# A second spare pair for split weights in the down projection of a hybrid decoder layer

## The chip, the cores and the metric

The kernel runs on one core of a Trainium2 chip. The core has five engines with instruction queues of their own: TensorE (PE in the profile; its weight loads are PEld), VectorE (DVE), ScalarE (ACT), GpSimd (POOL) and SyncE (SP), of which the last two issue transfers here. An engine takes its instructions in the order of the program and waits on semaphores. The metric is the time of one execution on the device, in microseconds; the median of three runs before is 2103.13 us (2101.62 to 2104.65).

## The reference

One decoder layer on x of 512 tokens by 2048, all in float32. With a token mixer (gated linear attention in 4 heads and differential attention in 4 heads) and a gated MLP:

```
h = rmsnorm(x, attn_pre_norm)
x = x + rmsnorm(token_mixer(h, ...), attn_post_norm)
h = rmsnorm(x, ffn_pre_norm)
up = h @ w_ffn_in                      # 2048 x 11264
a, b = up[..., :5632], up[..., 5632:]
a = conv_w[0]*a[t-2] + conv_w[1]*a[t-1] + conv_w[2]*a[t] + conv_b
f = (gelu(a) * b) @ w_ffn_out          # 5632 x 2048: the down projection
y = x + rmsnorm(f, ffn_post_norm)
```

The change concerns the last product, `@ w_ffn_out`.

## The kernel before

**Split weights.** TensorE works on operands of a rounded type (float32r). To keep float32 accuracy, each operand is split in two: ScalarE copies the raw tile into a rounded high half (line 137), VectorE subtracts that from the raw tile and writes the low half (line 138). A product is then three matmuls: high by high, high by low, low by high (lines 1348 to 1350 in the down projection). The unit of this work is the *granule*: 128 x 1024 weights, loaded in one transfer, split by one instruction on each of the two engines, and used by twelve matmuls of 128 x 512. `granule` does it, and takes the place of the two halves either from a *ring* of three slots (`halves`) or from a *spare pair* (`spare_halves`; tiles xhi and xlo, allocated once and kept in `kept`). Before TensorE has read a slot to the end, the next granule that has this slot can't be split. With every fourth granule in the spare pair, the ring and the pair make four slots in turn.

**The down projection.** The 11 groups of 512 hidden columns are taken as five pairs and one single group (`last_group`, at the end). Each pair, for each half of the 2048 output columns, is one *unit*: ten units, 0 to 9. A unit is a product of 2 x 2 blocks computed with seven block products instead of eight. Its segments are, in order, x0, z0, y0, z1, x1, y1, y2, of two granules each, so 14 granules or 168 matmuls; the order between units is chained (`x0` and `z0` of the next unit stand before and behind `y2` of this one). In this text 1/z0/0 is unit 1, segment z0, granule 0. The raw weights of a unit lie in three pairs of tiles: `rt` (segments x0, z0, y0, y2), a first pair of `raw` (z1, y1), and a second pair of `raw` (x1). Between its uses a tile is changed in place: after x0 and after z1 GpSimd issues a transfer that adds another weight block to it (`accum_op`, line 1194, and line 1454 in the hand-ordered part); before y0 and before y2 VectorE adds a `raw` tile to it (lines 1211 and 1229). The other operand of the products, the activations, comes from DRAM tiles `sd` as `st`, and is split into `ah` and `al` by ScalarE and VectorE (lines 150 and 151, a *preparation*); seven preparations belong to each pair of groups, so they fall between an odd unit and the even unit behind it. After each segment the banks are added to four accumulators `acc` (ScalarE copies the first of them, line 1354; VectorE adds, line 1356).

**What sets the order.** The step from the up projection to unit 1 is written by hand: `run_in_order` in a manual schedule, which ends with 0/y2/1. It takes its own list of spare granules (a local name `extra`), with every fourth granule of its later part in the spare pair; its last granule is one of these. From 1/z0/0 on, the flag `extra[0]` is set and the framework's scheduler orders each engine's instructions itself, by a model of their times, from the dependencies that the program order and the tiles give. `Unit.run` counts granules in `turn[0]` and asks for the spare pair.

**Tiles of the large pool.** Tiles of 128 x 2048 come from a pool of six places (tag t8). The up projection holds six split sums there; the four accumulators take four of the places at the change-over, and `g3` (the last norm's weights, 1 MB, loaded on SP's queue) takes the next free one.

Of the kernel before, what the change touches and what calls it, by code (L numbers as in the profile page):

```python
# [10 lines left out]
F32R = mybir.dt.float32r  # L11
# [19 lines left out]
GR = 1024  # L31
# [4 lines left out]
def hybrid_layer(ctx: ExitStack, tc: tile.TileContext, x, attn_pre_norm, w_in, w_alpha_up, b_alpha,  # L36
# [4 lines left out]
    x2, out2 = x[0], out[0]  # L41
# [58 lines left out]
    def load(src, a, by=None):  # L100
        raw = wpool.tile([P, GR], F32, name="raw", tag="raw", bufs=4)
        (by or nc.sync).dma_start(out=raw.rearrange("p (a b) -> p a b", a=a), in_=src)
        return raw
# [9 lines left out]
    def halves():  # L113
        slot[0] = (slot[0] + 1) % 3
        return [ring[:, RS * i + p:RS * i + p + GR] for i, p in zip((slot[0], slot[0] + 3), place_w[0])]

    kept = []

    def spare_halves(pool):
        if pool == "rt":  # L120
            return [rp.tile([P, GR], F32R, name=n, tag="rt", bufs=4) for n in ("xhi", "xlo")]
        if pool is True:
            if not kept:
                kept.extend(small_tile(n, F32R) for n in ("xhi", "xlo"))
            return kept
        return [pool.tile([P, GR], F32R, name=n, tag=n, bufs=4) for n in ("xhi", "xlo")]

    def granule(src, a, raw=None, spare=None, hl=None):
        if raw is None:
            raw = load(src, a)  # L130
        if hl is not None:
            hi, lo = hl[:, 0, :], hl[:, 1, :]
        elif spare:
            hi, lo = spare_halves(spare)
        else:
            hi, lo = halves()
        act(hi, raw, AF.Copy)  # L137
        tt(lo, raw, hi.bitcast(F32), ALU.subtract)  # L138
        r = "p (a b) -> p a b"
        return hi.rearrange(r, a=a), lo.rearrange(r, a=a)  # L140
# [932 lines left out]
    def small_tile(name, dt=F32):  # L1073
        return fp.tile([P, GR], dt, name=name, tag="t4", bufs=6)

    def large_tile(name, dt=F32):
        return fp.tile([P, D], dt, name=name, tag="t8", bufs=6)
# [88 lines left out]
    turn = [0]  # L1166
    extra = [False]

    class Unit:
# [12 lines left out]
        def run(self, seg, op, raws):  # L1182
            c, first = self.where(seg)
            if first:
                self.banks[c] = self.chain(c)
            for g in range(2):
                turn[0] += 1
                place_w[0] = APART if self.a == 4 else LEVEL
                hl = granule(None, self.a, raws[g], spare=extra[0] and turn[0] % 4 == 0)
                self.prods(self.banks[c], op, g, hl, first)  # L1190

        def more(self, raws, j):
# [464 lines left out]
```

## Time and profile before

| What | Value |
|---|---|
| median of the runs (lowest to highest) | 2103.13 us (2101.62 to 2104.65) |
| the profiled execution's own time | 2106.11 us |
| its span (first to last instruction) | 2104.4 us |
| mean granted clock of TensorE | 0.996 |
| TensorE busy between 1700 and 1800 us | 97.09 of 100 us |
| TensorE busy between 1800 and 1900 us | 98.75 of 100 us |
| TensorE busy between 1900 and 2000 us | 96.60 of 100 us |
| VectorE busy in these three stretches | 84.40, 82.05, 85.90 us |
| ScalarE busy in these three stretches | 51.91, 43.89, 44.51 us |

The profile shows one execution, in microseconds from the start of its span. A row of a timeline gives the start, the duration, the engine, the line, the operation, what it writes and reads, the count of equal instructions in a row, and in brackets the idle time of the engine before it with what ended it. A row of waits gives who waited for whom, then the total, the number and the longest. A row of stretches gives the length, then the busy time of PE, PEld, DVE, ACT and POOL with instruction counts, then the granted clock of TensorE (1.00 is full speed), the mean busy share of the DMA engines, and GB/s. Matmuls overlap: of two rows in a row the starts count, not the durations.

### The profile page before, as it was taken

What the parts mean: (1) busy time and instruction counts of PE and PEld (TensorE: products, weight loads), DVE (VectorE), ACT (ScalarE), POOL (GpSimd) and SP (SyncE); (2) the same over time, 40 slices, a digit from 0 to 9 for tenths busy, and PEclk for the clock granted to TensorE, in tenths of its full rate; (3) what the DMA queues carried; (4) which work ended last, traced back from release to release, by engine and by line L of the source; (5) the groups of instructions that cost most, each with busy time, mean ns of one, the idle gap of its engine ahead of it and who ended that gap; (6) DMA issues with size and microseconds to landing.
All of it is one profiled execution on the core that took longest, in us unless ns stands there. A gap on an engine that the chain in (4) does not pass through costs nothing.

```text
span 2104.4 us, 35571 instructions
## 1 busy us (share of the span) xinstructions
PE 2062.8 (98%) x14449; PEld 1903.4 (90%) x14449; DVE 1507.9 (72%) x1802; ACT 1001.9 (48%) x1306; POOL 287.5 (14%) x306
## 2 busy tenths in 40 slices
PE   7999999999989999999999999999999999999998
PEld 6699999999988889899999999999999878787786
DVE  5967777676752255986777767777777778888877
ACT  4544444455742233454554545455455554444443
POOL 0112222322200000011111011111111110110100
PEclk9999999999999999999999999999999999999999
DMA  5488887878875344447668577567676876776663
GB/s 210 118 185 179 191 197 176 178 176 198 196 193 175 100 150 161 140 103 196 150 147 196 140 162 190 135 163 175 164 160 179 239 208 168 192 189 159 171 169 140
DMA packets 280696, 358.60 MB, mean 170 GB/s; under 512 B 14592, under 2 KB 221876, under 8 KB 278612
## 3 DMA queue, kind: packets, MB, share of 16 engines
q1 hardware_dynamic: 191380, 259.85, 37.1%
q0 software_dynamic: 84800, 94.38, 29.6%
q8 instruction: 113, 1.85, 0.4%
q10 hardware_dynamic: 4352, 2.10, 0.3%
q14 instruction: 51, 0.42, 0.1%
HBM read 311.72 MB, written 44.56 MB: 169 GB/s over the span
## 4 chain that ended last, share of the span: by engine, by line
issue 37%; PE 29%; POOL 3%; DMA 2%; DVE 2%; ACT 1%; POOLq 0%; DVEq 0%; ACTq 0%; SPq 0%
PE bank L1248 4%; PE bank L1247 4%; PE bank L1246 4%; PE bank L191 3%; PE bank L192 3%; PE bank L193 3%; POOL raw L1194 1%; POOL rt L1194 1%; PE bank L1349 1%; PE bank L1350 1%; PE bank L1348 1%; PE bank L1553 1%; PE bank L1554 1%; PE bank L1552 1%; PE bank L175 1%
## 5 line engine op out<-in xcount | busy, mean ns | idle before, releaser
L138 DVE TENSOR_TENSOR ring<-raw,ring 128x1024 fp32r<-128x1024 f32 x315 | 383.1, 1221 | 280.8 <-ACT ring L137 276.5
L137 ACT ACTIVATE ring<-raw 128x1024 fp32r<-128x1024 f32 x315 | 333.3, 1060 | 516.4 <-PE bank L1247 119.7
L1248 PE MATMUL bank<-ah,ring 128*128 128x256 f32 x1280 | 353.4, 276 | 0.7 <-DVE ring L138 0.7
L1246 PE MATMUL bank<-ah,ring 128*128 128x256 f32 x1280 | 353.3, 276 | 0.0
L1247 PE MATMUL bank<-al,ring 128*128 128x256 f32 x1280 | 353.3, 276 | 0.0
L137 ACT ACTIVATE ring<-rt 128x1024 fp32r<-128x1024 f32 x221 | 233.2, 1060 | 247.3 <-PE bank L1247 146.1
L138 DVE TENSOR_TENSOR ring<-rt,ring 128x1024 fp32r<-128x1024 f32 x221 | 268.8, 1221 | 91.6 <-ACT ring L137 89.7
L1248 PEld LDWEIGHTS bank<-ah,ring 128*128 128x128 f32 x1280 | 240.3, 188 | 0.9 <-DVE ring L138 0.9
L1246 PEld LDWEIGHTS bank<-ah,ring 128*128 128x128 f32 x1280 | 240.3, 188 | 0.1
L1247 PEld LDWEIGHTS bank<-al,ring 128*128 128x128 f32 x1280 | 240.3, 188 | 0.1
L1349 PE MATMUL bank<-ring,ah 128*128 128x512 f32 x424 | 166.2, 392 | 6.3 <-DVE ring L138 6.3
L1350 PE MATMUL bank<-ring,al 128*128 128x512 f32 x424 | 165.1, 389 | 0.0
L1348 PE MATMUL bank<-ring,ah 128*128 128x512 f32 x424 | 158.6, 391 | 0.7 <-ACT ring L137 0.7
L192 PE MATMUL bank<-ring,ah 128*128 128x512 f32 x280 | 111.1, 398 | 0.8 <-DVE ring L138 0.8
L191 PE MATMUL bank<-ring,ah 128*128 128x512 f32 x280 | 110.5, 400 | 0.3 <-ACT ah L150 0.3
L193 PE MATMUL bank<-ring,al 128*128 128x512 f32 x280 | 110.0, 396 | 0.0
L1194 POOL DMA_DIRECT2D raw<-in_w_ffn_in_dram x40 | 51.2, 1309 | 397.2 <-DVE ring L138 397.2
L1349 PEld LDWEIGHTS bank<-ring,ah 128*128 128x128 f32 x424 | 79.6, 188 | 26.0 <-DVE ring L138 9.9
L1348 PEld LDWEIGHTS bank<-ring,ah 128*128 128x128 f32 x424 | 79.3, 188 | 19.8 <-ACT ring L137 3.2
L1194 POOL DMA_DIRECT2D rt<-in_w_ffn_in_dram x40 | 51.0, 1285 | 326.2 <-DVE ring L138 303.7
L1350 PEld LDWEIGHTS bank<-ring,al 128*128 128x128 f32 x424 | 79.6, 188 | 16.4
L746 PE MATMUL bank<-ring,ah 128*128 128x256 f32 x320 | 92.6, 289 | 0.0
(346 smaller groups left out, 5675.3 us busy)
## 6 DMA issues: line engine op xcount, KB each, us to landing
raw<-in_w_ffn_in_dram SPq DMA_DIRECT2D x96, 512.0 KB, 5.0
raw<-in_w_in_dram SPq DMA_DIRECT2D x56, 512.0 KB, 4.6
raw<-in_w_ffn_out_dram SPq DMA_DIRECT2D x48, 512.0 KB, 6.8
raw<-in_w_in_dram POOLq DMA_DIRECT2D x40, 512.0 KB, 7.2
rt<-in_w_ffn_in_dram SPq DMA_DIRECT2D x40, 512.0 KB, 5.9
rt<-in_w_ffn_in_dram POOLq DMA_DIRECT2D x40, 512.0 KB, 6.1
raw<-in_w_ffn_in_dram POOLq DMA_DIRECT2D x40, 512.0 KB, 6.8
raw<-in_w_o_dram SPq DMA_DIRECT2D x32, 512.0 KB, 3.9
```

The costliest lines, as they stand in the source:

```text
L137: act(hi, raw, AF.Copy)
L138: tt(lo, raw, hi.bitcast(F32), ALU.subtract)
L191: mm(banks[t], ah[:, t, s, :], w[0][:, k, :], start=st, stop=False)
L192: mm(banks[t], ah[:, t, s, :], w[1][:, k, :], start=False, stop=False)
L193: mm(banks[t], al[:, t, s, :], w[0][:, k, :], start=False, stop=sp)
L1194: nc.gpsimd.dma_start(out=raws[g].rearrange("p (a b) -> p a b", a=self.a), in_=self.block(0, j, g), accum_op=ALU.add)
L1246: mm(o, wh, sh[:, :, kk, :], start=start and kk == 0 and n == 0, stop=False, **NOW)
L1247: mm(o, wh, sl[:, :, kk, :], start=False, stop=False, **NOW)
L1248: mm(o, wl, sh[:, :, kk, :], start=False, stop=kk == HK - 1, **NOW)
L1348: mm(b[j], sh[:, o:o + P], w[0][:, q, :], start=start and st == 0, stop=False, **NOW)
L1349: mm(b[j], sh[:, o:o + P], w[1][:, q, :], start=False, stop=False, **NOW)
L1350: mm(b[j], sl[:, o:o + P], w[0][:, q, :], start=False, stop=st == 3, **NOW)
```

## The change

The kept spare pairs become a list. When `extra[0]` is set, which is from unit 1's z0 on, a second pair is allocated as one tile x2 of 128 x 2048 in the large pool; its halves are the high and the low part of a granule. The pairs are handed out in turn. And of five granules two now take a spare pair (where the count leaves 0 or 2 when divided by five), in place of one in four. So the ring's three slots and the two pairs make five slots in turn. The hand-ordered part keeps its one pair and its rule; the last group still asks once for a spare pair and gets one of the two. `g3` now takes the sixth place of the large pool and no longer the fifth.

```diff
         if pool is True:
             if not kept:
-                kept.extend(small_tile(n, F32R) for n in ("xhi", "xlo"))
-            return kept
+                kept.append([small_tile(n, F32R) for n in ("xhi", "xlo")])
+            if extra[0] and len(kept) == 1:
+                pair = large_tile("x2", F32R)
+                kept.append([pair[:, :GR], pair[:, GR:]])
+            kept.append(kept.pop(0))
+            return kept[-1]
...
                 place_w[0] = APART if self.a == 4 else LEVEL
-                hl = granule(None, self.a, raws[g], spare=extra[0] and turn[0] % 4 == 0)
+                hl = granule(None, self.a, raws[g], spare=extra[0] and turn[0] % 5 in (0, 2))
                 self.prods(self.banks[c], op, g, hl, first)
```

Every line behind the first part of the diff lies four lines further down in the changed kernel (line 137 is 141 there). The instructions are the same in number on every engine; up to the end of the hand-ordered part they also stand in the same order, but for the load of `g3`, which moves on SP's queue from ahead of unit 1's first preparations to behind the loads of unit 2's x0. From 1/z0/0 on the scheduler orders them anew.

The first place is ScalarE at the change-over. The tile rt_17064 is unit 1's first `rt` granule (1/z0/0, then 1/y0/0), rt_17066 the second (1/z0/1, then 1/y0/1); rt_16822 is 0/y2/1, raw_17300 or raw_17301 is 1/z1/0. Before:

```order
L137 ACTIVATE xhi_17071<-rt_16822 128x1024
L137 ACTIVATE ring_84<-rt_17064 128x1024
L1354 ACTIVATE acc0_16858<-bank_17213 128x512
L150 ACTIVATE ah_79<-st_17404 128x1024
L1354 ACTIVATE acc1_16859<-bank_17214 128x512
L137 ACTIVATE ring_84<-rt_17066 128x1024
L137 ACTIVATE ring_84<-rt_17064 128x1024
L1354 ACTIVATE acc2_16856<-bank_16930 128x512
L1354 ACTIVATE acc3_16857<-bank_16931 128x512
L137 ACTIVATE xhi_17071<-rt_17066 128x1024
L137 ACTIVATE ring_84<-raw_17300 128x1024
```

And now, on the same engine at the same place:

```order
L141 ACTIVATE xhi_17071<-rt_16822 128x1024
L141 ACTIVATE ring_84<-rt_17066 128x1024
L1358 ACTIVATE acc0_16858<-bank_17213 128x512
L154 ACTIVATE ah_79<-st_17405 128x1024
L1358 ACTIVATE acc1_16859<-bank_17214 128x512
L141 ACTIVATE x2_17270<-rt_17066 128x1024
L141 ACTIVATE ring_84<-raw_17301 128x1024
L1358 ACTIVATE acc2_16856<-bank_16930 128x512
L1358 ACTIVATE acc3_16857<-bank_16931 128x512
L141 ACTIVATE xhi_17071<-rt_17064 128x1024
L141 ACTIVATE ring_84<-rt_17064 128x1024
```

The split of 1/z0/0, the second row before, is the tenth row now and writes the pair that 0/y2/1 has just used; 1/z0/1, 1/y0/1 and 1/z1/0 stand ahead of it.

The second place is TensorE at the same point: the last matmuls of 0/y2/1 and the first of 1/z0/0 (banks 17268 and 17269). Before:

```order
L1348 MATMUL bank_16931<-xhi_17071,ah_79 128x512
L1349 MATMUL bank_16931<-xlo_17072,ah_79 128x512
L1350 MATMUL bank_16931<-xhi_17071,al_80 128x512
L1348 MATMUL bank_17268<-ring_84,ah_79 128x512
L1349 MATMUL bank_17268<-ring_84,ah_79 128x512
```

And now:

```order
L1352 MATMUL bank_16931<-xhi_17071,ah_79 128x512
L1353 MATMUL bank_16931<-xlo_17072,ah_79 128x512
L1354 MATMUL bank_16931<-xhi_17071,al_80 128x512
L1352 MATMUL bank_17268<-xhi_17071,ah_79 128x512
L1352 MATMUL bank_17269<-xhi_17071,ah_79 128x512
L1353 MATMUL bank_17268<-xlo_17072,ah_79 128x512
```

TensorE's order of granules has not moved: 1/z0/0 is still the first behind 0/y2/1, now from the spare pair.

The third place is VectorE between units 7 and 8, where raw_18804 (now raw_18805) is 7/y1/1, and rt_18946 and rt_18948 (now rt_18947 and rt_18949) are 8/x0/0 and 8/x0/1; rows into `acc` are evacuations, rows into `al` preparations. Before:

```order
L138 TENSOR_TENSOR ring_84<-raw_18802,ring_84 128x1024
L1356 TENSOR_TENSOR acc0_16858<-acc0_16858,bank_18770 128x512
L1356 TENSOR_TENSOR acc1_16859<-acc1_16859,bank_18771 128x512
L151 TENSOR_TENSOR al_80<-st_19050,ah_79 128x1024
L138 TENSOR_TENSOR ring_84<-raw_18804,ring_84 128x1024
L138 TENSOR_TENSOR ring_84<-rt_18946,ring_84 128x1024
L1356 TENSOR_TENSOR acc0_16858<-acc0_16858,bank_18874 128x512
L1356 TENSOR_TENSOR acc1_16859<-acc1_16859,bank_18875 128x512
L151 TENSOR_TENSOR al_80<-st_19090,ah_79 128x1024
L138 TENSOR_TENSOR xlo_17072<-rt_18948,xhi_17071 128x1024
```

And now:

```order
L142 TENSOR_TENSOR ring_84<-raw_18803,ring_84 128x1024
L142 TENSOR_TENSOR x2_17270<-raw_18805,x2_17270 128x1024
L1360 TENSOR_TENSOR acc0_16858<-acc0_16858,bank_18771 128x512
L1360 TENSOR_TENSOR acc1_16859<-acc1_16859,bank_18772 128x512
L155 TENSOR_TENSOR al_80<-st_19051,ah_79 128x1024
L142 TENSOR_TENSOR ring_84<-rt_18947,ring_84 128x1024
L142 TENSOR_TENSOR xlo_17072<-rt_18949,xhi_17071 128x1024
```

The two low halves of a segment now stand next to each other, and the evacuations and the preparation that stood ahead of the second one stand behind it.

## The prediction

> **What bounds the kernel now.** I read the page first, then the busy time by stretches of the down projection, then the waits of TensorE and ScalarE there, and last the timelines around its longest hole. Granules are named unit/segment/number, as above (1/z0/0 is unit 1, segment z0, first granule).
>
> ```profile
> span 2104.4 us, 35571 instructions
> PE 2062.8 (98%) x14449; PEld 1903.4 (90%) x14449; DVE 1507.9 (72%) x1802; ACT 1001.9 (48%) x1306; POOL 287.5 (14%) x306
> ```
> TensorE is the bound over the whole; the change touches only the stage from about 1697 us on.
>
> ```profile
> 1700.00:1730.00 30.00, 27.55 (x116) 21.64 (x117) 24.00 (x22) 19.79 (x26) 2.58 (x3) 1.00 0.64 179
> 1760.00:1790.00 30.00, 30.00 (x134) 24.86 (x133) 24.02 (x27) 13.59 (x14) 2.94 (x3) 1.00 0.65 170
> ```
> A full stretch of 30 us holds 134 matmuls (0.227 us each, 2.7 us for a granule's twelve); the first stretch holds 116. So TensorE does wait in this stage, a little. What for:
>
> ```profile
> PE bank L1349 <- DVE ring L138: 5.2, 6, 1.0
> PE bank L1349 <- DVE xlo L138: 2.0, 3, 0.8
> ACT ring L137 <- DMA rt<-in_w_ffn_out_dram: 51.3, 14, 8.9
> ACT ring L137 <- DMA raw<-in_w_ffn_out_dram: 48.4, 14, 5.8
> ACT ring L137 <- PE bank L1350: 23.2, 14, 3.7
> ```
> These are the waits between 1675 and 2060 us (total, times, longest): nine waits for the low half of a granule, 7.2 us. ScalarE, which makes the high halves, waits mostly for weights to land, 100 us in these rows, and 23 us for a ring slot that TensorE still reads. A further pair can only shorten the last kind directly.
>
> ```profile
> 1701.43 0.50 PE L1349 MATMUL bank<-ring,ah 128*128 128x512 f32 x1 [0.76 <-DVE ring L138]
> 1701.77 0.40 PE L1350 MATMUL bank<-ring,al 128*128 128x512 f32 x1
> 1702.00 0.40 PE L1348 MATMUL bank<-ring,ah 128*128 128x512 f32 x1
> 1704.16 0.50 PE L1348 MATMUL bank<-ring,ah 128*128 128x512 f32 x1
> 1705.42 0.50 PE L1349 MATMUL bank<-ring,ah 128*128 128x512 f32 x1 [0.76 <-DVE ring L138]
> 1728.40 0.50 PE L1349 MATMUL bank<-ring,ah 128*128 128x512 f32 x1 [0.76 <-DVE ring L138]
> 1745.48 0.50 PE L1349 MATMUL bank<-xlo,ah 128*128 128x512 f32 x1 [0.46 <-DVE xlo L138]
> ```
> The first row is 1/z0/0, the fifth 1/z0/1. A wait costs more than its idle figure: 1704.16 to 1705.42 is 1.26 us for a 0.23 us step, and the step behind a wait takes 0.34, so 1.14 us for 0.76 idle, that is idle + 0.38. After 1/z0/0 eight waits are left with 7.2 - 0.76 = 6.44 us idle, hence 6.44 + 8 x 0.38 = 9.5 us in all. That is the most the change can win. Of it 1.14 each lie in the rows at 1705 and 1728 and 0.84 at 1745, together 3.1; the other 6.4 come later, in units 4, 6 and 8 (a row of unit 8 stands under (4)).
>
> **The change part by part.**
>
> (1) More slots. Distance between two uses of a slot grows from four granules to five. No instruction is added or removed: the same splits write other addresses. A matmul from the present spare pair takes as long as one from the ring (0.50 each in the rows at 1745 and 1728, both behind a wait), so I price reading from the new pair at 0.
>
> (2) A clash at the change-over. The last granule of the hand-ordered part (0/y2/1) is in the old spare pair, and by the new rule so is the very next one, 1/z0/0. The scheduler answers, as the ScalarE order above shows, by putting 1/z0/0 eight instructions later, behind 1/z0/1, 1/y0/1, 1/z1/0, a preparation and four copies; TensorE's order still begins with 1/z0/0. How long TensorE then stands is worked out from these rows of ScalarE, VectorE and POOL:
>
> ```profile
> 1688.73 1.18 POOL L1454 DMA_DIRECT2D rt<-in_w_ffn_out_dram  x1 [15.20 <-DVE ring L138]
> 1691.05 1.19 POOL L1454 DMA_DIRECT2D rt<-in_w_ffn_out_dram  x1 [1.14 <-DVE ring L138]
> 1699.06 1.06 ACT L137 ACTIVATE ring<-rt 128x1024 fp32r<-128x1024 f32 x1 [8.95 <-DMA rt<-in_w_ffn_out_dram]
> 1700.03 0.58 ACT L1354 ACTIVATE acc<-bank 128x512 f32<-128x512 f32 x1
> 1700.51 1.05 ACT L150 ACTIVATE ah<-st 128x1024 fp32r<-128x1024 f32 x1
> 1701.45 0.59 ACT L1354 ACTIVATE acc<-bank 128x512 f32<-128x512 f32 x1
> 1703.04 2.01 ACT L137 ACTIVATE ring<-rt 128x1024 fp32r<-128x1024 f32 x2 [1.00 <-DMA rt<-in_w_ffn_out_dram]
> 1706.72 1.06 ACT L137 ACTIVATE xhi<-rt 128x1024 fp32r<-128x1024 f32 x1 [0.70 <-DVE rt L1211]
> 1707.69 1.04 ACT L137 ACTIVATE ring<-raw 128x1024 fp32r<-128x1024 f32 x1
> 1704.14 1.23 DVE L138 TENSOR_TENSOR ring<-rt,ring 128x1024 fp32r<-128x1024 f32 x1 [0.37 <-ACT ring L137]
> 1705.40 1.23 DVE L1211 TENSOR_TENSOR rt<-rt,raw 128x1024 f32<-128x1024 f32 x1
> ```
> The two accumulating transfers land at 1699.0 (first granule) and 1703.0 (second). Now the second is awaited first. ScalarE: 1/z0/1 at 1703.04; copy, preparation, copy end at 1705.9 (steps 0.97, 0.48, 0.94, 0.48 as in the rows); 1/y0/1 needs the sum on VectorE behind 1/z0/1's low half, so it starts at 1706.72 as the row of that kind does; 1/z1/0 at 1707.69; two copies from 1708.63; 1/z0/0 at 1709.6, done at 1710.65. VectorE: the low half of 1/y0/1 at 1707.8, a sum, the low half of 1/z1/0, then that of 1/z0/0, four steps of about 1.2, done near 1712.6. The matmul that stood at 1701.43 starts there: 11.2 us later. Bounds: the second transfer took 12.0 us from the start of its issue, the first 10.3; at 10.3 the term is 9.5.
>
> ```profile
> L48 SPq DMA_DIRECT2D g<-in_ffn_post_norm_dram x1: 419/419/419, 1665.0 to 1665.0; - x1
> DMA to landing us min/median/max: 5.1/5.1/5.1
> ```
> This 1 MB load (g3) moves on SP's queue from 1665 to behind the two loads of unit 2's x0, so into the flight of those two transfers; it landed in 5.1 us before, and if it shared fully, the term would be 16.3. I take 11.2, since it stands last in SP's queue behind 1 MB of older loads.
>
> (3) The clock after that hole. The trace has one comparable wait:
>
> ```profile
> PE bank L659 <- DVE on L652: 5.7, 1, 5.7
> 594.00:596.00 2.00, 0.00 (x0) 0.00 (x0) 1.17 (x2) 1.31 (x4) 0.88 (x2) 0.79 1.09 397
> 600.00:602.00 2.00, 2.00 (x11) 2.00 (x11) 1.61 (x2) 0.53 (x1) 0.00 (x0) 0.50 0.52 172
> 602.00:604.00 2.00, 2.00 (x20) 2.00 (x19) 0.10 (x1) 1.06 (x1) 0.00 (x0) 1.00 0.85 238
> 596.93 0.41 PE L746 MATMUL bank<-ring,in_s3h 128*128 128x256 f32 x1
> 601.63 0.41 PE L747 MATMUL bank<-ring,al 128*128 128x256 f32 x1
> 602.15 0.28 PE L747 MATMUL bank<-ring,al 128*128 128x256 f32 x1
> 605.10 0.28 PE L746 MATMUL bank<-ring,ah 128*128 128x256 f32 x1
> ```
> After 5.7 us of waiting the granted clock is 0.50 until about 601.9, and matmuls come every 0.214 us (22 steps between the first two matmul rows) in place of 0.1135 (26 steps between the last two). From 596.4 that is 5.5 us at about half pace: 2.6 us lost. A hole of 11 us is longer, so +2.6; bounds 0 (clock kept) and 3.2 (a stretch of 6.4 us).
> The Trainium skill, page "TensorE: Matmul & The Clock Gate", section Part 1 on the HAM clock gate, has the same mechanism with a shorter stretch: half rate after about 3.4 us idle, until about 3.4 us of activity. By that figure the loss would be an estimated 1.7 us and the sum below 0.9 lower.
>
> (4) What the hole gives back. TensorE is 13.8 us late behind it (11.2 + 2.6) while loads and splits go on. The waits at 1705, 1728 and 1745, whose weights then wait for TensorE, go: -3.1. The lost lead of the later units is rebuilt; whether it lasts is the question of slots:
>
> ```profile
> 1960.89 1.06 ACT L137 ACTIVATE ring<-raw 128x1024 fp32r<-128x1024 f32 x1 [4.94 <-DMA raw<-in_w_ffn_out_dram]
> 1977.94 1.06 ACT L137 ACTIVATE xhi<-rt 128x1024 fp32r<-128x1024 f32 x1 [4.00 <-DMA rt<-in_w_ffn_out_dram]
> 1754.01 1.06 ACT L137 ACTIVATE ring<-raw 128x1024 fp32r<-128x1024 f32 x1 [1.88 <-PE bank L1350]
> ```
> The first two rows are the chain of a later stall: an accumulating transfer lands, its granule is split, the next accumulating transfer depends on it; slots play no part there. The third row is a split of unit 2 that waited for a slot: there the lead of the splits is capped at three granules. So the waits come back every two units, 6.4 us in three pairs, 2.1 us for a pair. The cap rises by one granule, 2.7 us, more than a pair loses; so I let the later waits go. Against it stands the new order on VectorE (the third place above): evacuations and preparations that filled its waiting for a transfer now stand behind the awaited granule, so the chain itself is not shorter. I keep one wait of 1.1 us in unit 8, where the lead is smallest: -5.3. Bounds: 0 and -6.4.
>
> (5) g3 itself is read only in the last group; its later load costs nothing beyond (2). The end of the kernel keeps its order.
>
> **The sum**: +11.2 + 2.6 - 3.1 - 5.3 = +5.4 us. It is made against the profiled execution (2106.11 us, of which 2104.4 are the span), which lies 3.0 us above the median of the runs; I put the difference on the median: 2103.1 + 5.4 = 2108.5 us.
>
> **Rivals.**
>
> A. The later waits stay, because they come from the chain of transfers and not from slots. For it: 100 us of waiting for weights against 23 for slots, and VectorE's new order. Against it: the third row under (4), and a lead of 13.8 us handed over by the hole. Time: +11.2 + 2.6 - 3.1 = +10.7, 2113.8 us.
>
> B. Faster: the hole does not open and all waits go, -9.5, 2093.6 us at best. The one mechanism is the time at which the second accumulating transfer lands: the sum without any later wait is hole + 2.6 - 9.5, so it is under -4.2 us only for a hole below 2.7 us, that is a landing near 1694.5, some 2 us after its issue ended at 1692.2. The two rows of its kind took 10.3 and 12.0 us. For it speaks only that nothing else in the order is worse.
> The Trainium skill, page "Perfetto Trace Analysis", section "Optimization Strategy", says that the same gap repeating on an engine that should be saturated can mean too little room for the next tile; by it the waits of units 4, 6 and 8 are of that kind, and the room given would remove them. The ScalarE waits above put only the smaller part on slots.
>
> C. g3 collides with the two transfers: the hole is 16.3 us, the rest as forecast, +10.5, 2113.6 us. For it: it is issued while both are in flight. Against it: older loads stand ahead of it in SP's queue.
>
> That the pair is not used can be left out: the order shows x2 written and read.
>
> **How the numbers follow.** 0.2% is 4.2 us, about what a measurement of this kernel can tell from no change. The forecast's case (the hole as worked out, most later waits gone) gets 0.68, A 0.20, C 0.07, B 0.05. Inside the forecast's case the time runs from +1.3 (hole 9.5, clock 1.3, halfway between its bound of 0 and the row, all waits gone) to +8 (half of the later waits left); a bit over a third of it lies under +4.2. So faster 0.05, same 0.26, slower 0.69. Likeliest 2108.5 us; the case's own range is 2104.4 to 2111; taking in A and C up to their values, 2104 to 2114.
>
> **What would show it.** (2): one wait of TensorE of 9 to 13 us near 1700, released by ScalarE and VectorE on xhi and xlo, with y0/1 on x2 split before z0/0; wrong if no wait above 3 us stands there. (3): granted clock near 0.5 for some 5 us behind it. (4): no wait at the places of 1705, 1728 and 1745; in units 4, 6 and 8 at most one or two waits of 1 us; wrong, and A right, if pairs of waits of about 1 us still stand there. ScalarE's waits for TensorE (23 us) should shrink. The prediction is wrong as a whole if the transfers at the change-over land much sooner or later than at 1703, or if the new VectorE order opens waits in the odd units that were not there.

## The result, and the profile after

The changed kernel takes 2119.92 us (median of five runs, 2113.57 to 2125.42), the kernel before 2102.38 us in the runs beside it: 1.0084 times as long, 95% interval 1.0068 to 1.0100. It is 17.5 us slower; forecast were 5.4 us, with 2114 us as the upper end.

The head of the page, of the profiled execution (2119.86 us):

```profile
span 2118.1 us, 35569 instructions
PE 2061.6 (97%) x14449; PEld 1903.5 (90%) x14449; DVE 1509.8 (71%) x1802; ACT 1003.9 (47%) x1306; POOL 287.6 (14%) x306
```

All busy times are those of before within 2 us, so the 13.7 us by which the two spans differ are not added work (the profiled execution of before lay some 4 us above its median, this one at it). What TensorE waits for in the down projection, from 1675 to 2060 us:

```profile
PE bank L1352 <- ACT xhi L141: 11.1, 1, 11.1
PE bank L1352 <- DVE acc L1360: 9.2, 4, 4.0
PE bank L1353 <- DVE ring L142: 1.2, 2, 0.8
PE bank L1353 <- DVE xlo L142: 0.7, 1, 0.7
```

The first row is one hole at the change-over. The second is of a kind that before has nowhere in this stage: four waits for an evacuation. Of the nine small waits for low halves three are left, one in the hole and two in unit 6. Two stretches of 30 us:

```profile
1700.00:1730.00 30.00, 22.63 (x86) 18.02 (x87) 23.69 (x21) 18.61 (x24) 2.36 (x2) 0.77 0.55 149
1970.00:2000.00 30.00, 26.03 (x102) 20.92 (x101) 27.16 (x30) 15.33 (x16) 2.39 (x2) 0.89 0.52 139
```

The first stretch has 86 matmuls (116 before), at a granted clock of 0.77. The second also lost clock.

**The hole.** TensorE around it, then the clock behind it in steps of 2 us:

```profile
1695.17 0.39 PE L1354 MATMUL bank<-xhi,al 128*128 128x512 f32 x1
1706.67 1.22 PE L1352 MATMUL bank<-xhi,ah 128*128 128x512 f32 x2 [11.11 <-ACT xhi L141]
1708.59 0.79 PE L1353 MATMUL bank<-xlo,ah 128*128 128x512 f32 x1 [0.70 <-DVE xlo L142]
...
1713.45 0.46 PE L1353 MATMUL bank<-ring,ah 128*128 128x512 f32 x1
```

```profile
1706.00:1708.00 2.00, 1.22 (x2) 0.50 (x2) 2.00 (x3) 0.61 (x1) 0.00 (x0) 0.50 0.21 86
1712.00:1714.00 2.00, 2.00 (x7) 1.51 (x7) 0.14 (x1) 0.69 (x1) 0.00 (x0) 0.61 0.89 122
1714.00:1716.00 2.00, 2.00 (x10) 1.67 (x9) 1.60 (x2) 0.98 (x3) 0.00 (x0) 1.00 0.78 140
```

And its source on POOL (the second accumulating transfer) and on ScalarE:

```profile
1687.21 1.19 POOL L1458 DMA_DIRECT2D rt<-in_w_ffn_out_dram  x1 [1.14 <-DVE ring L142]
```

```profile
1699.08 1.06 ACT L141 ACTIVATE ring<-rt 128x1024 fp32r<-128x1024 f32 x1 [13.34 <-DMA rt<-in_w_ffn_out_dram]
...
1705.56 1.05 ACT L141 ACTIVATE xhi<-rt 128x1024 fp32r<-128x1024 f32 x1
```

From the issue at 1687.21 the transfer took 11.9 us (12.0 before), and 1/z0/0 is split 6.5 us behind 1/z0/1. From that issue to the first matmul with the low half TensorE took 21.4 us, before 10.4: the hole costs 11.0 us.

**The new waits.** The longest stands at 7/y2, whose first matmul needs 7/y1's evacuation, since both use the same banks. TensorE, ScalarE and VectorE there:

```profile
1979.56 0.39 PE L1354 MATMUL bank<-xhi,al 128*128 128x512 f32 x1
1983.91 0.77 PE L1352 MATMUL bank<-ring,ah 128*128 128x512 f32 x1 [3.97 <-DVE acc L1360]
```

```profile
1977.44 2.01 ACT L154 ACTIVATE ah<-st 128x1024 fp32r<-128x1024 f32 x2 [5.22 <-DMA st<-ud]
```

```profile
1978.54 2.36 DVE L155 TENSOR_TENSOR al<-st,ah 128x1024 fp32r<-128x1024 f32 x2 [2.10 <-ACT ah L154]
1980.81 2.35 DVE L142 TENSOR_TENSOR ring<-rt,ring 128x1024 fp32r<-128x1024 f32 x2
1983.08 1.28 DVE L1360 TENSOR_TENSOR acc<-acc,bank 128x512 f32<-128x512 f32 x2
```

Between the evacuations of x1 and y1 VectorE has two preparations and both low halves of y2. Before, it has four rows there too (two preparations, a low half of 8/x0 and one of y2), and did them from 1965.45 to 1969.99 us without a wait. Now the first of the four is the preparation that waits for its load, 2.10 us, so what the load and what the order costs at this place is not told apart. The other three waits are at 4/z1, 5/z1 and 6/z1, behind z0's evacuation.

**The balance.** The count of matmuls between 1720 and 2050 us tells what is lost behind the change-over. Undisturbed, 330 us hold 1457 of them (a run below has just that). The kernel before, then the changed one:

```profile
1720.00:2050.00 330.00, 324.13 (x1416) 264.31 (x1415) 273.70 (x294) 146.99 (x147) 37.83 (x32) 1.00 0.70 180
```

```profile
1720.00:2050.00 330.00, 319.54 (x1391) 262.17 (x1390) 269.71 (x287) 147.33 (x148) 38.20 (x32) 0.99 0.65 171
```

Before lost 41 matmuls, 9.3 us at 0.227 us each; the changed kernel lost 66, 15.0 us. The 15.0 us are: four waits for evacuations, 9.2 us idle with some 0.3 more each (the wait at 1837 took 1.64 us from start to start for 1.25 idle, and the step behind it 0.34 in place of 0.23), 10.4 together; half clock behind the longest, where thirteen steps from 1984.47 to 1990.02 took 5.55 us in place of 2.95, 2.6; and the two small waits in unit 6, 2.0. So 5.7 us are added behind the change-over, where the forecast had taken 7.3 us away (1.14 + 0.84 of the waits at 1728 and 1745, 5.3 of the later ones). With the hole (11.0) and the half clock behind it (2.4, below), less the old wait at 1705 that the hole swallowed (1.1), this makes 18.0 us, against 17.5 between the medians.

### The profile page after: what moved, and what is told of

Read it like the earlier page. It is cut to its first block, busy times and chain, and to the rows that moved or that the text cites. A ratio compares the mean times of both kernels' runs of the same rounds, so it can differ in the third digit from the quotient of the medians.

```text
span 2118.1 us, 35569 instructions
## 1 busy us (share of the span) xinstructions
PE 2061.6 (97%) x14449; PEld 1903.5 (90%) x14449; DVE 1509.8 (71%) x1802; ACT 1003.9 (47%) x1306; POOL 287.6 (14%) x306
## 5 line engine op out<-in xcount | busy, mean ns | idle before, releaser
L142 DVE TENSOR_TENSOR ring<-raw,ring 128x1024 fp32r<-128x1024 f32 x307 | 374.1, 1223 | 279.0 <-ACT ring L141 278.5
L141 ACT ACTIVATE ring<-raw 128x1024 fp32r<-128x1024 f32 x307 | 324.9, 1060 | 496.6 <-PE bank L1251 117.0
L1252 PE MATMUL bank<-ah,ring 128*128 128x256 f32 x1280 | 353.4, 276 | 0.0
L1250 PE MATMUL bank<-ah,ring 128*128 128x256 f32 x1280 | 353.3, 276 | 0.0
L141 ACT ACTIVATE ring<-rt 128x1024 fp32r<-128x1024 f32 x210 | 222.2, 1061 | 248.0 <-PE bank L1251 146.6
L142 DVE TENSOR_TENSOR ring<-rt,ring 128x1024 fp32r<-128x1024 f32 x210 | 256.0, 1222 | 89.7 <-ACT ring L141 89.5
L1352 PE MATMUL bank<-ring,ah 128*128 128x512 f32 x348 | 136.7, 395 | 7.9 <-DVE acc L1360 7.9
L1353 PE MATMUL bank<-ring,ah 128*128 128x512 f32 x348 | 137.4, 395 | 2.4 <-DVE ring L142 2.4
L1354 PE MATMUL bank<-ring,al 128*128 128x512 f32 x348 | 136.5, 392 | 0.0
L196 PE MATMUL bank<-ring,ah 128*128 128x512 f32 x280 | 109.5, 392 | 0.3 <-DVE ring L142 0.2
L195 PE MATMUL bank<-ring,ah 128*128 128x512 f32 x280 | 109.2, 395 | 0.0
L197 PE MATMUL bank<-ring,al 128*128 128x512 f32 x280 | 108.6, 391 | 0.0
L750 PE MATMUL bank<-ring,ah 128*128 128x256 f32 x320 | 92.1, 288 | 0.0
L746 PE MATMUL bank<-ah,ring 128*128 128x256 f32 x320 | 90.8, 284 | 0.0
L751 PE MATMUL bank<-ring,al 128*128 128x256 f32 x320 | 89.4, 280 | 0.0
L752 PE MATMUL bank<-ring,ah 128*128 128x256 f32 x320 | 89.3, 279 | 0.0
```

Of the source, the lines that this page charges most:

```text
L195: mm(banks[t], ah[:, t, s, :], w[0][:, k, :], start=st, stop=False)
L196: mm(banks[t], ah[:, t, s, :], w[1][:, k, :], start=False, stop=False)
L197: mm(banks[t], al[:, t, s, :], w[0][:, k, :], start=False, stop=sp)
L1250: mm(o, wh, sh[:, :, kk, :], start=start and kk == 0 and n == 0, stop=False, **NOW)
L1252: mm(o, wl, sh[:, :, kk, :], start=False, stop=kk == HK - 1, **NOW)
L1352: mm(b[j], sh[:, o:o + P], w[0][:, q, :], start=start and st == 0, stop=False, **NOW)
```

## The experiments

The runs ask three things: whether the new waits come from the hole (e1, e2), whether from the slots or from the order of VectorE and ScalarE (e3, e5 to e8), and which rows of the order do it (e4, e9 to e16). Each kernel is compared with the kernel before, run beside it on the same chip. Its median was 2104.1 us beside e1 to e4, 2102.4 beside e5 to e8 and 2102.6 beside the others.

**e1: the clash taken away.**

```diff
-                kept.append([pair[:, :GR], pair[:, GR:]])
+                kept.insert(0, [pair[:, :GR], pair[:, GR:]])
```

> The changed kernel with one edit: the new pair is handed out first, so 1/z0/0 takes x2 and not the pair that 0/y2/1 still occupies. The order of the rest stays that of the changed kernel, with both splits of z1 and of y2 ahead of the evacuation that these products wait for. Theory O (the order on VectorE makes the new waits for evacuations, the clash makes the hole): no hole at the change-over, so 11.0 + 2.6 us less than the changed kernel, about 2106 us, and three to five waits for evacuations of 1 to 4 us stay in units 4 to 7. Rival L (the waits for evacuations follow from TensorE being 13.6 us late behind the hole): they vanish with it, no wait for an evacuation above 0.5 us, and the time lies between 2093 and 2102 us.

Measured: 2118.68 us, 1.0071 (1.0059 to 1.0084). The hole is gone, yet the time is nearly that of the changed kernel, some 13 us over what theory O gave. The waits for evacuations are more:

```profile
PE bank L1352 <- DVE acc L1360: 11.1, 6, 2.6
```

So L falls: the waits don't need the hole. Five stand at z1 of units 2 to 6, the sixth at 7/y2. VectorE ahead of one of them, at 2/z1 (PE's row stands last):

```profile
1743.96 1.23 DVE L142 TENSOR_TENSOR x<-rt,x 128x1024 fp32r<-128x1024 f32 x1 [2.45 <-ACT x L141]
1745.10 1.28 DVE L1360 TENSOR_TENSOR acc<-acc,bank 128x512 f32<-128x512 f32 x2
1746.30 1.22 DVE L1215 TENSOR_TENSOR rt<-rt,raw 128x1024 f32<-128x1024 f32 x1
1747.44 2.52 DVE L142 TENSOR_TENSOR ring<-rt,ring 128x1024 fp32r<-128x1024 f32 x2
1749.87 2.35 DVE L1233 TENSOR_TENSOR rt<-rt,raw 128x1024 f32<-128x1024 f32 x2
1752.14 1.22 DVE L155 TENSOR_TENSOR al<-st,ah 128x1024 fp32r<-128x1024 f32 x1
1753.28 1.22 DVE L142 TENSOR_TENSOR xlo<-raw,xhi 128x1024 fp32r<-128x1024 f32 x1
1754.41 1.22 DVE L142 TENSOR_TENSOR ring<-raw,ring 128x1024 fp32r<-128x1024 f32 x1
1755.55 1.28 DVE L1360 TENSOR_TENSOR acc<-acc,bank 128x512 f32<-128x512 f32 x2
```

```profile
1756.28 0.50 PE L1352 MATMUL bank<-xhi,ah 128*128 128x512 f32 x1 [1.72 <-DVE acc L1360]
```

The first row is the low half of 2/z0/1, released late, since its transfer was late. From here TensorE has three granules to do (z0/1, y0/0, y0/1: 8.2 us) before it needs z0's banks again for z1. VectorE has queued 11.5 us of rows up to the end of that evacuation, so it comes too late. I call these rows the *stretch* of a unit. For unit 4 the order gives this stretch in the kernel before and in the changed one as follows (by the steps in the rows above, 1.14 us for a row of 128 x 1024 and 0.60 for the evacuation of one bank):

| | rows behind the low half of z0/1, up to the end of z0's evacuation | sum |
|---|---|---|
| before | addition for y0/1, low half y0/0, evacuation of 3/y2 (2 banks), addition for y2/0, preparation, low halves y0/1 and z1/0, z0's evacuation with the addition for y2/1 in the middle | 10.4 us |
| changed, and e1 | 4/x0's evacuation (2 banks), addition for y0/1, low half y0/0, evacuation of 3/y2 (2), low half y0/1, additions for y2/0 and y2/1, preparation, low halves z1/0 and z1/1, z0's evacuation | 12.7 us |

Over units 2 to 9 the stretch is 9.5 us in the mean before, 12.7 in the changed kernel and in e1.

**e2: the clash alone.** One pair as before, one granule later in the count.

```diff
-                hl = granule(None, self.a, raws[g], spare=extra[0] and turn[0] % 4 == 0)
+                hl = granule(None, self.a, raws[g], spare=extra[0] and turn[0] % 4 == 1)
```

> The kernel before, with the one old pair, every fourth granule in it as before, but one granule later in the count, so that 1/z0/0 follows 0/y2/1 in the same pair. There is no second pair, and the order on VectorE puts one split and not two ahead of the evacuations, as before. Theory O: a hole of about 11 us near 1700 us, half clock behind it, and no new wait for an evacuation: +11.0 + 2.6 for the two, -3.1 for the waits at 1705, 1728 and 1745, about 2113 us. Rival L (lateness behind the hole brings the waits for evacuations): the same hole and also waits for evacuations, 2118 to 2122 us.

Measured: 2110.76 us, 1.0031 (1.0019 to 1.0042), 6.6 us over before. TensorE's waits from 1675 us on:

```profile
PE bank L1348 <- ACT xhi L137: 10.6, 1, 10.6
```

The hole and no wait for an evacuation, as O said; VectorE's stretch is that of before. Between 1720 and 2050 us:

```profile
1720.00:2050.00 330.00, 327.53 (x1442) 270.26 (x1441) 277.78 (x296) 151.46 (x151) 39.01 (x33) 1.00 0.68 179
```

That is 15 matmuls short of 1457, 3.4 us, where before lost 9.3. So with the four slots of before, TensorE's lateness behind the hole takes away 5.9 us of the waits; the prediction gave it only the two at 1728 and 1745, 2.0 us, and the later ones to the slots.

**e3: two pairs, still one granule in four.**

```diff
-                hl = granule(None, self.a, raws[g], spare=extra[0] and turn[0] % 5 in (0, 2))
+                hl = granule(None, self.a, raws[g], spare=extra[0] and turn[0] % 4 == 0)
```

> The changed kernel with both pairs in turn, but still every fourth granule in a pair, so the ring's slots come back after four granules as before. 1/z0/0 is in the ring, so there is no clash. VectorE's order has one split ahead of z0's evacuation, as before. Theory O: no hole, no wait for an evacuation above 1 us, the small waits for low halves remain: 2099 to 2104 us. Rival X (the tile x2 itself is slow to write or to read, or the load of g3 at its later place disturbs): 2105 us or more with longer splits or matmuls on x2.

Measured: 2099.95 us, 0.9982 (0.9973 to 0.9990): 4.2 us faster than before. Rival X falls: the tile x2 and the later load of g3 cost nothing that shows. Nor does reading from it, in the changed kernel itself (matmuls from x2, and from the ring):

```profile
L1353 PE MATMUL bank<-x,ah 128*128 128x512 f32 x96 | 37.4, 389 | 0.0
```

```profile
L1353 PE MATMUL bank<-ring,ah 128*128 128x512 f32 x292 | 115.1, 394 | 1.2 <-DVE ring L142 1.2
```

**e4: two rows moved behind the evacuation.** Edges of issue order, no waits:

```diff
+                behind[0] = self.done.get({"z1": "z0", "y2": "y1"}.get(seg)) if extra[0] and g == 1 else None
                 hl = granule(None, self.a, raws[g], spare=extra[0] and turn[0] % 5 in (0, 2))
...
+        low = tt(lo, raw, hi.bitcast(F32), ALU.subtract)
+        if behind[0] is not None:
+            issue_behind(low, behind[0])
```

> The new pair first, as in the run before the last two, and two edges of order for each unit: on VectorE the low half of z1's second granule is issued behind z0's evacuation, and the low half of y2's second granule behind y1's. Nothing else is changed. Theory O: the waits for evacuations go or shrink below 1 us, and what is left is at or below the kernel before: 2095 to 2102 us. Rival D (the evacuations come late because VectorE as a whole falls behind, whatever the order of two rows): waits for evacuations of 1 us and more stay, 2104 us or more.

Measured: 2124.48 us, 1.0095 (1.0080 to 1.0109), worse than without the edges. TensorE's waits, 1720 to 2050 us:

```profile
PE bank L1362 <- DVE acc L1370: 6.4, 6, 1.5
PE bank L1363 <- DVE ring L148: 4.0, 6, 1.2
```

The waits for evacuations shrank, and waits for low halves came. By its order the scheduler had answered the two edges by moving other rows: in unit 4, for one, the first addition for y0 now stood behind the awaited low half of z0/1 as well, where x0's evacuation already stood in e1, and ahead of y0/0. The stretch was still 12.0 us in the mean, and y0/0 was late too. So the result is not read as a verdict on the evacuation alone.

**e5, e6: order and slots apart.** The instructions of VectorE and ScalarE are held to a given order: to that of the kernel before, with five slots (e5), and to that of e1, with the four slots of the kernel before (e6).

```diff
+        free = nc.cur_bb.bb.instructions[n0:]
+        for engine, seq in ORDER.items():
+            mine = [i for i in free if i.engine == engine]
+            for earlier, later in zip(seq, seq[1:]):
+                tc.add_manual_dep(mine[later], mine[earlier].name, ...
```

> Five slots without the clash (the new pair first, two of five granules in a pair), but on VectorE and ScalarE the instructions of the down projection are issued in exactly the order that they have in the kernel before. Theory O (the loss of the run with the new pair first, 14.6 us over the kernel before, comes from the new order of VectorE and ScalarE): the loss is gone, 2098 to 2104 us, no wait for an evacuation above 1 us. Rival S (the loss comes from the five slots themselves: from reading and writing them, or from the transfers that they let start sooner): 2113 to 2120 us, as with the new order.

> The other corner: the kernel before with its four slots and one pair, but VectorE and ScalarE issue in the order that the scheduler made for five slots (that of the run with the new pair first). Theory O: the order carries the loss, 2115 us or more, with waits for evacuations at z1 and y2. Rival S: the time stays with the slots, 2100 to 2106 us.

Measured: e5 2104.02 us, 1.0003 (0.9993 to 1.0014); e6 2116.75 us, 1.0065 (1.0051 to 1.0079). The matmuls between 1720 and 2050 us, e5 and e6:

```profile
1720.00:2050.00 330.00, 323.71 (x1414) 264.43 (x1413) 274.78 (x295) 146.12 (x149) 37.82 (x32) 1.00 0.68 178
```

```profile
1720.00:2050.00 330.00, 317.71 (x1365) 258.40 (x1364) 267.98 (x286) 144.57 (x144) 38.16 (x32) 0.98 0.65 171
```

With the slots changed and the order kept the loss is that of before (43 matmuls, 9.8 us); with the order changed and the slots kept it is 92, 20.9 us. The loss goes with the order, and S falls. That five slots in the old order gain nothing is no surprise: an order made for four puts no split further ahead.

**e7: the clash in the old order.** The changed kernel, with both engines held to the order of before.

> The changed kernel with its clash (1/z0/0 in the pair of 0/y2/1), but VectorE and ScalarE in the order of the kernel before, so 1/z0/0 is still split ahead of 1/z0/1, right behind 0/y2/1's last copies. Theory O: the hole came from the eight places by which the split was moved, not from the shared pair: it shrinks to 2 to 5 us, no half clock behind it, no waits for evacuations, 2100 to 2106 us. Rival P (the shared pair itself makes the hole, whatever the order): 8 to 12 us of hole and half clock, 2108 to 2114 us.

Measured: 2102.92 us, 1.0003 (0.9992 to 1.0013). At the change-over TensorE waits

```profile
1696.14 0.73 PE L1376 MATMUL bank<-xhi,ah 128*128 128x512 f32 x2 [1.63 <-ACT xhi L165]
```

1.6 us in place of 11.1. So the shared pair as such is harmless; the eight places by which the split of 1/z0/0 was moved made the hole.

**e8: another phase of two in five.**

```diff
-                hl = granule(None, self.a, raws[g], spare=extra[0] and turn[0] % 5 in (0, 2))
+                hl = granule(None, self.a, raws[g], spare=extra[0] and turn[0] % 5 in (0, 3))
```

> The new pair first and two of five granules in a pair, but where the count leaves 0 or 3 (and not 2) when divided by five: the same number of slots, no clash, other granules in the pairs. Theory O: the scheduler again sets both splits ahead of the evacuations, so the loss repeats: 2114 to 2122 us. Rival F (the loss belongs to the particular granules that stand in the pairs, as with the first rule): within 4 us of the kernel before.

Measured: 2113.15 us, 1.0053 (1.0039 to 1.0067), a microsecond under the range of O. The stretch is 12.7 us again, and six waits for evacuations between 1720 and 2050 us take 12.5 us. The loss is not that of particular granules.

**e9, e10: one engine's order alone.** As e5, with only VectorE (e9) or only ScalarE (e10) held to the order of before.

> Five slots, the new pair first; only VectorE is held to the order of the kernel before, ScalarE's order is left to the scheduler. Theory V (the loss sits in VectorE's order): 2099 to 2106 us, no wait for an evacuation above 1 us. Rival A (it sits in ScalarE's order of the splits): 2112 us or more.

> The mirror of the run before: only ScalarE is held to the order of the kernel before, and the scheduler orders VectorE around it. In the odd units VectorE's rows between the low half of z0's second granule and the end of z0's evacuation then amount to 9.2 us as before, in the even units to 12.7 or 13.9 us as in the changed kernel. Theory V: about half the loss is left, 2106 to 2113 us, with waits for evacuations in the even units alone. Rival A: 2099 to 2105 us.

Measured: e9 2126.89 us, 1.0118 (1.0100 to 1.0135), the slowest of all; e10 2106.36 us, 1.0020 (1.0007 to 1.0032). Theory V as worded for e9 was wrong. VectorE's waits in e9, and a row of ScalarE in it:

```profile
DVE al L171 <- ACT ah L170: 31.6, 9, 5.8
```

```profile
1896.95 1.06 ACT L157 ACTIVATE x<-raw 128x1024 fp32r<-128x1024 f32 x1 [7.76 <-PE bank L1370]
```

In ScalarE's new order a split that has to wait for a slot stands ahead of a preparation that VectorE's old order wants first: the two orders belong together, and VectorE stood 31.6 us for preparations alone. In e10 the scheduler fitted VectorE to ScalarE's old order, and most of the loss went; but no wait for an evacuation stayed, though the stretch of the even units from 2 to 8 is 12.7 to 13.9 us there as expected. So a long stretch alone does not make the wait; in e10 TensorE waits for low halves instead, 7.6 us between 1720 and 2050 us.

**e11: four edges on VectorE.** The new pair first (as e1). The first addition for y0 and x0's evacuation are issued ahead of the low half of z0/1; the low half of z1/1 and the addition for y2/1 behind z0's evacuation.

```diff
+                if g == 0 and self.done.get("x0"):
+                    issue_behind(self.low["z0", 1], add, self.done["x0"])
...
+                if g == 1 and self.done.get("z0"):
+                    issue_behind(late, self.done["z0"])
+                    issue_behind(self.low["z1", 1], self.done["z0"])
```

> Five slots, the new pair first, both engines ordered by the scheduler but for four edges in each unit on VectorE: the first addition for y0 and x0's evacuation stand ahead of the low half of z0's second granule, which waits for a transfer; the low half of z1's second granule and the second addition for y2 stand behind z0's evacuation. VectorE's rows between that low half and the end of the evacuation fall from 12.7 to 9.2 us. Theory V, in its narrow form (these rows make the wait): the waits for z0's evacuation go, and with them most of the loss: 2101 to 2108 us; the waits at y2 may stay. Rival W (the loss is spread over the whole order): 2112 us or more.

Measured: 2098.00 us, 0.9982 (0.9972 to 0.9991): 4.6 us under before, where e1 lay 14.6 over the before of its own chip, so 19.1 us between the two. The stretch is 9.1 us, and TensorE waits for nothing between 1720 and 2050 us:

```profile
1720.00:2050.00 330.00, 330.00 (x1457) 273.36 (x1456) 281.88 (x301) 151.58 (x151) 37.92 (x32) 1.00 0.68 183
```

What was set is the place of four rows in each unit, though the scheduler moved others on account of them: 47 of VectorE's 306 rows of units 1 to 9 stand elsewhere than in e1. W falls. The wait at 7/y2 is gone too, with both low halves of y2 still ahead of y1's evacuation and no edge on them: VectorE is no longer late there (that evacuation starts at 1961.91 us, y2 at 1966.60).

**e12: one in four, another phase.** As e3, with the new pair first and the count's remainder 2.

> Both pairs, every fourth granule, where the count leaves 2 when divided by four (0 in the third run), the new pair first; no clash. Theory V: the rows between the low half and the end of z0's evacuation are 11.5 us in half of the units (9.2 in the third run) and short in the others, so some waits return: 2102 to 2110 us. Rival G (the gain of the third run belongs to one in four as such): 2097 to 2102 us.

Measured: 2106.71 us, 1.0023 (1.0011 to 1.0034). The gain of e3 is not that of one in four as such. The stretches in this expectation were miscounted, since in these two orders the granule of z0 that lands last is not always the same; counted from that one, they are 10.3 to 12.7 us here (mean 12.0) and 9.2 to 11.6 in e3 (mean 10.4). Nor do the waits follow them: units 3, 5 and 7 have 12.7 us and no wait for an evacuation, and the only one, 1.9 us, is at 8/z1.

**e13, e14: the four edges on four slots, and with the clash.** e13 is the kernel before with e11's edges, e14 the changed kernel with them.

> The four edges of the run before, but on the kernel before with its one pair and four slots. Theory C (the five slots are worth something once the order is right): the waits for low halves of units 4, 6 and 8 stay as in the kernel before, 2101 to 2105 us, about 5 us above the run with five slots and the edges. Rival N (the second pair is worth nothing, the four edges alone make the gain): 2097 to 2100 us.

> The four edges on the changed kernel itself, clash included: 1/z0/0 in the pair of 0/y2/1 and split eight places later. Theory H (the clash has a price of its own, the one forecast: 11.0 + 2.6 us of hole and half clock, less the 3 to 5 us of waits behind it that fall away): 2098 us + 9 to 11, so 2106 to 2110 us. Rival Z (the price is hardly seen, as between the changed kernel and the run with the new pair first, 1.2 us apart): 2098 to 2101 us.

Measured: e13 2103.15 us, 0.9999 (0.9990 to 1.0007); e14 2105.45 us, 1.0011 (1.0003 to 1.0020). In e13 43 matmuls are missing between 1720 and 2050 us, 41 in before; the small waits stay, some of them for ScalarE now:

```profile
PE bank L1362 <- DVE ring L145: 2.8, 4, 1.0
PE bank L1361 <- ACT ring L144: 1.6, 4, 0.8
...
```

So the five slots, with the order that the scheduler makes for them under the edges, are worth 5.1 us (e11 against e13), and N falls. In e14 the hole of 10.2 us is the only wait of the down projection above 1 us; its price is 7.5 us (e14 against e11), below the 9 to 11 of theory H: e11 has five waits at 1/z0 and just behind it, 4.15 us idle and 0.38 more for each, some 6 us that the hole swallows.

**e15, e16: the edges in two halves.** e15 has only the two ahead of z0/1's low half, e16 only the two behind z0's evacuation.

> The new pair first, with the first two of the four edges alone: x0's evacuation and the first addition ahead of the awaited low half. The rows between it and the end of z0's evacuation then amount to 11.5 us (12.7 without edges, 9.2 with all four). Theory V: in proportion, about a third of the gain of 20 us: 2109 to 2115 us, with waits for z0's evacuation left. Rival T (TensorE's three granules there last 8.2 us, and whatever exceeds its lead counts fully, so the first rows count most): below 2105 us.

> The other two edges alone: the low half of z1's second granule and the second addition for y2 behind z0's evacuation; the rows amount to 10.4 us. Theory V: two thirds of the gain, 2103 to 2108 us, few waits for evacuations. Rival M (moved behind the evacuation they only delay the next granules, as the two edges of the fourth run did): 2112 us or more.

Measured: e15 2097.07 us, 0.9973 (0.9962 to 0.9984); e16 2098.72 us, 0.9981 (0.9973 to 0.9990). The matmuls between 1720 and 2050 us, e15 and e16:

```profile
1720.00:2050.00 330.00, 329.10 (x1451) 272.00 (x1450) 281.05 (x301) 151.18 (x153) 37.97 (x32) 1.00 0.68 183
```

```profile
1720.00:2050.00 330.00, 326.95 (x1435) 268.79 (x1434) 277.75 (x298) 148.51 (x149) 38.02 (x32) 1.00 0.66 179
```

Either half is enough. V's proportion falls, and M with it; T's time for e15 came out, but not its reason, that the first rows count most, since the other two rows do as well alone. A stretch of 11.4 us (e15) loses 6 matmuls there, 1.4 us, one of 10.4 (e16) 22, 5.0 us, one of 12.7 (e1) 81, 18.4 us. e16 is the narrowest of the mended kernels: against e1 22 of VectorE's 306 rows and one instruction of ScalarE stand elsewhere. e15 has the lowest median of this study, 22.9 us under the changed one; its interval overlaps those of e11 and e16.

## Why the prediction was wrong

- **Step (1), more slots, the new pair read at no price: right.** e3 and the matmul rows show it.
- **Step (2), the hole of 11.2 us: right.** 11.0 us in the changed kernel, at the place and by the chain named. That the cause is the order and not the pair, e7 shows.
- **Step (3), 2.6 us of half clock: right.** From 1708.59 to 1713.45 eleven matmuls took 4.86 us in place of 2.50, 2.4 us lost. The granted clock was 0.50 or mixed from 1706.67 until about 1713.5, 6.8 us. The Trainium skill, page "TensorE: Matmul & The Clock Gate", Part 1 on the HAM clock gate, gives about 3.4 us for such a stretch; behind this hole the trace does not agree, and the loss by that figure, 1.7 us, was too low (behind the short wait in the last section half clock lasted about 3.5 us).
- **Step (4), waits given back, -3.1 and -5.3, with no price for the new order: the step that failed.** Its sentence that VectorE's new order stands against the gain was the right place to look, but it took the order to leave the chain "not shorter" and priced no wait for an evacuation. That is the missing term: in the changed kernel four such waits cost 10.4 us and the half clock behind the longest 2.6, 13.0 us where the sum had nothing; 5.4 and 13.0 make 18.4, against 17.5 measured. Without the clash the new order costs 19.1 us (e1 against e11). The gain itself came out in size: of the 9.3 us that before loses between 1720 and 2050 us, 2.0 are left in small waits, where the sum kept 1.1. The waits at 1705, 1728 and 1745 went, and those of units 4 and 8. But that the slots did it is right only in part. With four slots the lateness behind the hole takes 5.9 of the 9.3 us (e2), with five slots and the mended order all of it goes (e14: 1457 matmuls). Without a hole the five slots are worth 5.1 us in the time (e11 against e13); that this lies near the 5.3 of the sum is partly luck, since e13 loses 9.8 us between 1720 and 2050 us and e11 nothing, while e11 waits more at the change-over. With the order mended and the clash left in, e14 comes to 2.8 us over before, where the sum was +5.4. So slower was forecast rightly, but of the 17.5 us most is a term that the sum did not have.
- **Step (5), g3's later load at 0: right**, the transfer took 11.9 us as before, so rival C did not happen. Rival A did not happen either: of the waits that it kept, those of units 4 and 8 are gone, and of unit 6 two of 0.76 and 0.47 us still stand, at z0/1 and y0/0. Rival B needed a transfer landed near 1694.5; it landed at 1699.1. The rule of the Trainium skill behind it, page "Perfetto Trace Analysis", section "Optimization Strategy", that a repeating gap can mean too little room for the next tile, is borne out by e11 against e13: with a fifth slot the repeated gaps of units 4, 6 and 8 go. It holds under the condition that the order of the other engines lets the room be used: in the old order (e5) 43 matmuls are still lost with five slots.

What these 19.1 us are made of, in e1: six waits of 11.1 us idle, some 0.3 us more for each (1.8), and three stretches at half clock, around 1798, 1921 and 1986 us, at 1.7 us or less each (the last section). These make up to 18 us; the 81 matmuls missing between 1720 and 2050 us are 18.4.

The prediction had named the sign that would make it wrong as a whole (new waits in odd units), without a price for it; they stand in units 4 to 7. A warning, though no price, could have been had from the order: the stretch was 9.5 us before and 12.7 now, against 8.2 us of matmuls plus TensorE's lag behind VectorE.

What stays open: that the order of VectorE's rows makes the loss is shown by e5, e6, e11, e15 and e16, but the stretch is only a rough measure of it. Why the edge lies near 12 us is argued from e1's rows only (at 2/z1 TensorE could have gone on 10.4 us after the low half began, and did after 12.3). Units with 12.7 us and more go without the wait in e10 and e12, e9 is the slowest with the stretch of before, and e16 loses more than e15 with a shorter one. The wait at 7/y2 has a late load in it. Why the scheduler puts two low halves ahead of an evacuation when there is a fifth slot was not tried.

## What to carry to other kernels

Room for one more tile is also a new order of every engine, where a scheduler makes it: before pricing the room, list for each wait of the bounding engine what the serving engine has queued ahead of it, before and after, and sum it against the time that the bounding engine has there; a long sum is a place to look, not yet a price. In an engine that works in order a row that waits is a gate (in e9 VectorE stood 31.6 us at preparations): what others wait for belongs ahead of it, what nobody waits for yet behind. And when two buffers change hands at a change-over, look which instruction the scheduler delayed on account of it, since that, and not the sharing, was the price of the hole here.

## What the runs showed of the hardware

A short wait can cost half a granted clock, and it need not. In e1 a wait of 2.05 us was followed by matmuls every 0.43 us; TensorE, and the clock in two steps behind it:

```profile
1796.69 0.77 PE L1352 MATMUL bank<-ring,ah 128*128 128x512 f32 x1 [2.05 <-DVE acc L1360]
...
1799.39 0.63 PE L1352 MATMUL bank<-ring,ah 128*128 128x512 f32 x1
1799.82 0.51 PE L1353 MATMUL bank<-ring,ah 128*128 128x512 f32 x1
```

```profile
1798.00:1800.00 2.00, 2.00 (x6) 1.52 (x6) 2.00 (x3) 0.00 (x0) 0.00 (x0) 0.50 1.06 190
1802.00:1804.00 2.00, 2.00 (x10) 1.69 (x9) 2.00 (x2) 0.23 (x1) 0.00 (x0) 1.00 1.06 283
```

Eight matmuls took 3.48 us (1796.69 to 1800.17) in place of 1.81, 1.7 us lost. The wait of 1.72 us at 1756.28, shown with e1, was followed by full pace, but so was a longer one in the changed kernel:

```profile
1920.18 0.50 PE L1352 MATMUL bank<-ring,ah 128*128 128x512 f32 x1 [2.65 <-DVE acc L1360]
```

And in e6 a wait of 1.82 us, at 1754.76, was followed by steps of 0.43 us from 1755.89 on. So a wait of about 2 us may cost most of its own length again, or nothing, and no threshold can be read from these runs. The Trainium skill, page "TensorE: Matmul & The Clock Gate", Part 1 on the HAM clock gate, puts the drop behind an idle window of about 3.4 us; the drop after 2.05 us does not agree with that as a bound.
